# One row of the first load on eleven and nine DMA engines instead of sixteen, in a softmax with relative position bias

## The chip, the cores and the metric

The kernel runs on one core of a Trainium2 chip. The metric is device time in microseconds (us), the median of several runs. A core has compute engines that each run their own instruction stream: VectorE (DVE in the profile), ScalarE (ACT), GpSimd (POOL), TensorE (PE, not used here) and SyncE (SP), which here only issues transfers. Transfers between HBM and the on-chip memory (SBUF, 128 partitions) are carried by 16 DMA engines. Semaphores order everything: a transfer adds 16 to its semaphore when all of its data has landed.

## The reference

```
logits: (2, 8, 2112, 2112) float32      rel_bias: (8, 33) float32

rel  = pos[:, None] - pos[None, :]                  # 2112 x 2112
bias = rel_bias[:, clip(rel, -16, 16) + 16]         # one band matrix per head
x    = logits + bias[None]
x    = x - x.max(axis=-1, keepdims=True)
out  = exp(x) / exp(x).sum(axis=-1, keepdims=True)
```

There are 2 x 8 x 2112 = 33,792 rows of 2112 numbers (8448 bytes each). Each row gets a bias that depends only on the distance to its own position, and then a softmax. The input is 285 MB, the output as much.

## The kernel before, in words

Each of the 128 partitions owns 264 consecutive rows (ROWS). The kernel walks through them in 44 chunks of R = 6 rows per partition. A chunk is 128 partitions x 6 rows x 8448 bytes = 6336 KB, and one partition's part of it is contiguous in HBM. Four SBUF buffers X[0] to X[3] (NBUF) hold chunks in rotation; all work on a chunk is done in place.

For each chunk, VectorE adds the bias and takes the row's maximum in one instruction per row (line 167), ScalarE takes the exponential and the row's sum (line 176), VectorE inverts the sums (line 184) and scales the rows (line 188), half a chunk at a time. The bias is read from a strip F that is copied once per four chunks out of a longer band M in PSUM (`strip`, line 161). M is made in the first microseconds from `rel_bias`, by small VectorE instructions (lines 118 to 157).

SyncE issues all large transfers, in an order that is written out by hand. It first issues the first chunk as six loads of one row per partition (lines 88 to 91), then chunks 1 to 3 as one load each (lines 92 and 93, `load`, line 79). Then, in a loop, it waits for a chunk to be scaled and issues its store (`store`, line 83), waits until the store before it has landed, and issues the load that reuses that buffer (line 209). The last chunk is stored in two halves (lines 212 and 213). `take` (line 75) is the wait everywhere: it waits until a semaphore has reached a count and takes that count off again.

Two semaphores tell of the first chunk. The first five row loads count on `pre`, the sixth on `ld[0]`, which later loads of buffer 0 use too. VectorE waits for `pre` before its loop, and so before the first strip copy (line 191):

```
take(v, pre, 16 * (R - 1))
```

It then copies the strip, and waits for `ld[0]` (in `add`) before the first addition.

Of the kernel before, what the change touches and what calls it, by code (L numbers as in the profile page):

```python
# [15 lines left out]
def kernel(  # L16
# [6 lines left out]
    nc = tc.nc  # L23
    P = 128
    B, H, S, S2 = logits.shape
# [3 lines left out]
    ROWS = B * H * S // P  # L29
    PB = S // ROWS  # L30
    assert ROWS * P == B * H * S and PB * ROWS == S and PB == H == 8
    R = 6
# [5 lines left out]
    MW = S + ROWS - 1  # L38
    FW = S + STEP - 1
    BIG = 3.0e38  # L40

    io = ctx.enter_context(tc.tile_pool(name="io", bufs=1))
    X = [io.tile([P, R * S], FP32, tag=f"X{b}", name=f"X{b}") for b in range(NBUF)]
# [9 lines left out]
    def view(t, offset, dims):  # L53

        return bass.AP(tensor=t.tensor, offset=t.offset + offset, ap=[[list(t.ap[0])[0], P]] + dims)

    def rows(t, j, n):

        return bass.AP(tensor=t.tensor, offset=t.offset + j * S, ap=[[ROWS * S, P], [1, n * S]])

    with tc.tile_critical(no_gpsimd_drain=True):
        ld = [nc.alloc_semaphore(f"ld{b}") for b in range(NBUF)]
# [6 lines left out]
        pre = nc.alloc_semaphore("pre")  # L69
# [4 lines left out]
        def take(eng, sem, n):  # L74
            eng.wait_ge(sem, n).then_inc(sem, -n)  # L75
# [9 lines left out]
            ).then_inc(sem or st[b], 16)  # L85


        for r in range(R):
            nc.sync.dma_start(
                out=X[0][:, r * S : (r + 1) * S], in_=rows(logits, r, 1)  # L90
            ).then_inc(ld[0] if r == R - 1 else pre, 16)
        for n in range(1, NBUF):
            load(n * R, n)

# [4 lines left out]
            out=rbB,  # L99
            in_=bass.AP(tensor=rel_bias.tensor, offset=rel_bias.offset, ap=[[0, P], [1, H * W]]),  # L100
# [4 lines left out]
        v = nc.vector  # L105
# [22 lines left out]
        for m, op in ((eq, ALU.is_equal), (gt, ALU.is_gt), (le, ALU.is_le), (lt, ALU.is_lt)):  # L128
# [4 lines left out]
            out=view(F, 0, [[W, H], [1, W]]), in0=view(F, 0, [[W, H], [1, W]]),  # L133
# [9 lines left out]
            out=view(F, 0, [[W, PB], [1, W]]), in0=view(F, SC + 2 * PB, [[1, PB], [0, W]]),  # L143
# [7 lines left out]
            out=view(M, U, [[ROWS, PB], [1, W]]), in0=view(F, 0, [[W, PB], [1, W]]),  # L151
            in1=view(F, SC + 8 * PB, [[1, PB], [0, W]]), op=ALU.add))
        then(v.tensor_copy(out=view(M, U + W, [[ROWS, PB], [1, ROWS - W]]),  # L153
                           in_=view(F, SC + 7 * PB, [[1, PB], [0, ROWS - W]])))
# [8 lines left out]
        def add(b):  # L163
            take(v, ld[b], 16)
            for r in range(b * R, (b + 1) * R):
                x = X[b][:, (r - b * R) * S : (r - b * R + 1) * S]
                v.tensor_tensor_reduce(  # L167
                    out=x, in0=x, in1=F[:, STEP - 1 - r : STEP - 1 - r + S], scale=-1.0, scalar=BIG,
                    op0=ALU.add, op1=ALU.min, accum_out=nmax[:, r : r + 1],
# [18 lines left out]
                    v.tensor_scalar_mul(out=x, in0=x, scalar1=rec[:, r : r + 1]).then_inc(scaled, 1)  # L188

        v.sem_inc(dve, -done[0])  # L190
        take(v, pre, 16 * (R - 1))
        with nc.Fori(0, ROWS - STEP + 1, STEP, engines=[ENG.DVE]) as j:  # L192
            strip(j)
            take(v, dve, 1)
# [52 lines left out]
```

## Time and profile before

| | |
|---|---|
| median of 3 runs | 1331.21 us (1329.54 to 1332.16) |
| the profiled execution | 1330.01 us, its span 1328.2 us |
| VectorE busy | 976.7 us (74%) |
| ScalarE busy | 575.2 us (43%) |
| DMA queue of SP (q1) | 99.6% of 16 engines' span |
| moved over the span | 571.11 MB, 430 GB/s in the mean |
| loads of a chunk, issue to landing | 44.8 us median |
| stores of a chunk, issue to landing | 52.7 us median |

The span runs from the first to the last instruction of the profiled execution; its own time is a little longer. A DMA share is the mean busy share of the 16 DMA engines, so that 0.50 over a stretch can mean eight engines that work all the time. In lists of instructions, a trailing bracket names how long the engine was idle before, and what ended the wait. A `q` after an engine's name (SPq, DVEq) is its sequencer, which issues transfers and waits on semaphores.

### The profile page before, as it was taken

What the parts mean: (1) busy time and instruction counts of PE and PEld (TensorE: products, weight loads), DVE (VectorE), ACT (ScalarE), POOL (GpSimd) and SP (SyncE); (2) the same over time, 40 slices, a digit from 0 to 9 for tenths busy, and PEclk for the clock granted to TensorE, in tenths of its full rate; (3) what the DMA queues carried; (4) which work ended last, traced back from release to release, by engine and by line L of the source; (5) the groups of instructions that cost most, each with busy time, mean ns of one, the idle gap of its engine ahead of it and who ended that gap; (6) DMA issues with size and microseconds to landing.
All of it is one profiled execution on the core that took longest, in us unless ns stands there. A gap on an engine that the chain in (4) does not pass through costs nothing. (4 is left out here: it accounts for less than half of the span.)

```text
span 1328.2 us, 2456 instructions
## 1 busy us (share of the span) xinstructions
DVE 976.7 (74%) x911; ACT 575.2 (43%) x539; POOL 0.4 (0%) x6
## 2 busy tenths in 40 slices
DVE  6999667777877776687778777677877776677772
ACT  2574333444444343344444333434444343335441
POOL 0000000000000000000000000000000000000000
DMA  9999999999999999999999999999999999999998
GB/s 395 429 426 438 429 430 435 429 432 430 435 435 432 427 437 437 432 432 429 437 437 427 430 437 437 430 427 440 437 434 429 435 437 435 430 432 438 434 430 357
DMA packets 13682, 571.11 MB, mean 430 GB/s; under 512 B 1520, under 2 KB 1648, under 8 KB 1648
## 3 DMA queue, kind: packets, MB, share of 16 engines
q1 hardware_dynamic: 13536, 570.96, 99.6%
q10 hardware_dynamic: 144, 0.14, 0.1%
q14 instruction: 2, 0.02, 0.0%
HBM read 285.61 MB, written 285.47 MB: 430 GB/s over the span
## 5 line engine op out<-in xcount | busy, mean ns | idle before, releaser
L167 DVE CUSTOM_DVE_ANT_0 X<-X,F 128x2112 f32<-128x2112 f32 x264 | 605.2, 2354 | 302.1 <-DVEq L75 302.1
L176 ACT ACTIVATE X<-X,nmax 128x2112 f32<-128x2112 f32 x264 | 541.7, 2052 | 540.9 <-ACTq L75 519.2
L188 DVE TENSOR_SCALAR X<-X,rec 128x2112 f32<-128x2112 f32 x264 | 332.4, 1315 | 13.2
L176 ACT ACT_TABLE_LOAD x11 | 14.1, 1283 | 182.5 <-ACTq L75 182.5
L176 ACT ACTIVATION_READ_ACCUMULATOR X<-X,nmax 128x1 f32 x264 | 49.3, 187 | 0.0
L161 DVE COPY F<-M 128x2135 f32 x11 | 26.1, 2374 | 6.3 <-DVEq L75 6.3
L167 DVE DVE_READ_ACCUMULATOR2_ANT nmax<- 128x1 f32 x264 | 21.7, 82 | 0.0
L184 DVE RECIPROCAL rec<-tot 128x3 f32<-128x3 f32 x88 | 15.0, 170 | 0.0
L132 DVE TENSOR_TENSOR F<-F 128x264 f32<-128x264 f32 x1 | 0.4, 434 | 4.6 <-DMA F<-in_rel_bias_dram 4.6
L153 DVE COPY M<-F 128x1848 f32<-128x1848 f32 x1 | 2.1, 2077 | 0.0
L119 DVE TENSOR_SCALAR ip<-ip 128x8 int32<-128x8 int32 x1 | 0.2, 172 | 1.3 <-POOL ip L103 1.3
L136 DVE TENSOR_REDUCE rbS<-F 128x33 f32<-128x264 f32 x1 | 0.6, 611 | 0.0
L150 DVE TENSOR_TENSOR M<-F 128x264 f32<-128x264 f32 x1 | 0.4, 441 | 0.0
L142 DVE TENSOR_TENSOR F<-F,rbS 128x264 f32<-128x264 f32 x1 | 0.4, 428 | 0.0
L129 DVE TENSOR_SCALAR F<-F 128x8 f32<-128x8 f32 x4 | 0.4, 167 | 0.0
L155 DVE COPY M<-rbS 128x247 f32<-128x247 f32 x1 | 0.4, 406 | 0.0
L140 DVE TENSOR_SCALAR F<-F,rbS 128x8 f32<-128x8 f32 x1 | 0.2, 231 | 0.0
L146 DVE SCALAR_TENSOR_TENSOR F<-F,rbS 128x8 f32<-128x8 f32 x1 | 0.2, 225 | 0.0
L141 DVE TENSOR_SCALAR F<-F,rbS 128x8 f32<-128x8 f32 x1 | 0.2, 226 | 0.0
L147 DVE SCALAR_TENSOR_TENSOR F<-F,rbS 128x8 f32<-128x8 f32 x1 | 0.2, 219 | 0.0
L122 DVE TENSOR_TENSOR F<-ip 128x8 f32<-128x8 int32 x1 | 0.2, 168 | 0.0
L125 DVE TENSOR_TENSOR F<-ip 128x8 f32<-128x8 int32 x1 | 0.2, 168 | 0.0
(9 smaller groups left out, 1.2 us busy)
## 6 DMA issues: line engine op xcount, KB each, us to landing
X<-in_logits_dram SPq DMA_DIRECT2D x43, 6336.0 KB, 44.8
out_dram<-X SPq DMA_DIRECT2D x43, 6336.0 KB, 52.7
X<-in_logits_dram SPq DMA_DIRECT2D x6, 1056.0 KB, 12.0
out_dram<-X SPq DMA_DIRECT2D x2, 3168.0 KB, 21.1
F<-in_rel_bias_dram ACTq DMA_DIRECT2D x1, 132.0 KB, 6.2
```

The lines of the kernel that those rows point to most:

```text
L129: then(v.tensor_scalar(out=m, in0=dp, scalar1=0.0, scalar2=None, op0=op))
L132: then(v.tensor_tensor(out=view(F, 0, [[W, H], [1, W]]), in0=view(F, 0, [[W, H], [1, W]]), in1=view(F, SC + 3 * PB, [[1, H], [0, W]]), op= ...
L136: then(v.tensor_reduce(out=rbS[:, :], in_=view(F, 0, [[1, W], [W, H]]), axis=mybir.AxisListType.X, op=ALU.add))
L142: then(v.tensor_tensor(out=view(F, 0, [[W, PB], [1, W]]), in0=view(F, SC + 2 * PB, [[1, PB], [0, W]]), in1=view(rbS, W - 1, [[0, PB], [-1, ...
L150: then(v.tensor_tensor(out=view(M, U, [[ROWS, PB], [1, W]]), in0=view(F, 0, [[W, PB], [1, W]]), in1=view(F, SC + 8 * PB, [[1, PB], [0, W]] ...
L153: then(v.tensor_copy(out=view(M, U + W, [[ROWS, PB], [1, ROWS - W]]), in_=view(F, SC + 7 * PB, [[1, PB], [0, ROWS - W]])))
L155: then(v.tensor_copy(out=M[:, 0:U], in_=low.to_broadcast([P, U])))
L161: v.tensor_copy(out=F[:, :], in_=M[:, bass.ds(ROWS - STEP - j, FW)]).then_inc(dve, 1)
L167: v.tensor_tensor_reduce(out=x, in0=x, in1=F[:, STEP - 1 - r : STEP - 1 - r + S], scale=-1.0, scalar=BIG, op0=ALU.add, op1=ALU.min, accum_ ...
L176: nc.scalar.activation(out=x, in_=x, func=EXP, scale=-1.0, bias=nmax[:, r : r + 1], accum_out=tot[:, r : r + 1],).then_inc(expd, 1)
L184: v.reciprocal(out=rec[:, r0 : r0 + HALF], in_=tot[:, r0 : r0 + HALF]).then_inc(inv, 1)
L188: v.tensor_scalar_mul(out=x, in0=x, scalar1=rec[:, r : r + 1]).then_inc(scaled, 1)
```

## The change

The sixth row of the first chunk is loaded by two transfers in place of one: partitions 0 to 109, and partitions 110 to 127. They carry the same bytes to the same places. The 128-partition transfer has eight partitions for each of 16 DMA engines; the one of 110 runs on eleven engines with ten partitions each, the one of 18 on nine engines with two each. The first of the two counts on `pre`, which VectorE awaits before the strip copy, and the second on `ld[0]`, so that `pre` now stands for 16 x 6. Everything behind is as before.

```diff
+    MOST = 11 * 10
...
-        for r in range(R):
+        for r in range(R - 1):
             nc.sync.dma_start(
                 out=X[0][:, r * S : (r + 1) * S], in_=rows(logits, r, 1)
-            ).then_inc(ld[0] if r == R - 1 else pre, 16)
+            ).then_inc(pre, 16)
+        for p0, p1 in ((0, MOST), (MOST, P)):
+            nc.sync.dma_start(
+                out=X[0][p0:p1, (R - 1) * S : R * S],
+                in_=bass.AP(
+                    tensor=logits.tensor, offset=logits.offset + (p0 * ROWS + R - 1) * S,
+                    ap=[[ROWS * S, p1 - p0], [1, S]],
+                ),
+            ).then_inc(ld[0] if p1 == P else pre, 16)
...
-        take(v, pre, 16 * (R - 1))
+        take(v, pre, 16 * R)
```

## The prediction

> **What bounds the kernel now.** I read the page's busy shares and slices first, then its queues, then the stretches at both ends, and last what the issuing queue waits for.
>
> ```profile
> span 1328.2 us, 2456 instructions
> ...
> DVE 976.7 (74%) x911; ACT 575.2 (43%) x539; POOL 0.4 (0%) x6
> ...
> DMA  9999999999999999999999999999999999999998
> ...
> q1 hardware_dynamic: 13536, 570.96, 99.6%
> ```
>
> No compute engine is near full, while the 16 DMA engines are at work for 99.6% of the span: one queue of loads and stores, never empty until the last slice. The stretches say how fast it runs (columns: stretch, its length, DVE, ACT and POOL busy, clock, DMA share, GB/s).
>
> ```profile
> 7.00:17.00 10.00, 4.93 (x11) 0.00 (x0) 0.00 (x0) 1.00 1.01 427
> ...
> 900.00:1300.00 400.00, 297.38 (x275) 179.09 (x169) 0.00 (x0) 1.00 1.00 434
> ```
>
> 434 GB/s over sixteen engines is 27.1 GB/s each. There is no idle engine time in the body, so a byte put on one engine costs that engine its full time, and the kernel ends when the slowest of the 16 ends. That they do not end together is what the last microseconds show.
>
> ```profile
> 1320.00:1321.00 1.00, 0.00 (x0) 0.00 (x0) 0.00 (x0) 1.00 0.88 380
> 1321.00:1322.00 1.00, 0.00 (x0) 0.00 (x0) 0.00 (x0) 1.00 0.53 228
> 1322.00:1323.00 1.00, 0.00 (x0) 0.00 (x0) 0.00 (x0) 1.00 0.47 203
> 1323.00:1324.00 1.00, 0.00 (x0) 0.00 (x0) 0.00 (x0) 1.00 0.41 177
> 1324.00:1325.00 1.00, 0.00 (x0) 0.00 (x0) 0.00 (x0) 1.00 0.35 152
> 1325.00:1326.00 1.00, 0.00 (x0) 0.00 (x0) 0.00 (x0) 1.00 0.18 76
> 1326.00:1327.00 1.00, 0.00 (x0) 0.00 (x0) 0.00 (x0) 1.00 0.06 25
> 1327.00:1328.00 1.00, 0.00 (x0) 0.00 (x0) 0.00 (x0) 1.00 0.00 0
> ```
>
> Every engine has the same bytes in this kernel. Yet from 1321 to 1322 only 0.53 x 16, about 8.5, are still working, and in the last busy microsecond 0.06 x 16, one. So half of the engines end near 1321 and the other half straggle, the last to about 1327, 6 us later. The seven shares sum to 2.88 us: had all sixteen ended together, that would have been at 1320 + 2.88 = 1322.9, 4.1 us earlier. Where the stragglers lose it is seen in the queue that issues the loads. A load is issued as soon as the store before it on its buffer has landed on the last engine, so these starts follow the slowest engine (the view is the timeline of SP's own queue: start, length, name).
>
> ```profile
> 157.14 0.35 SPq L79 DMA_DIRECT2D X<-in_logits_dram  x1
> ...
> 278.19 0.35 SPq L79 DMA_DIRECT2D X<-in_logits_dram  x1
> ...
> 908.83 0.35 SPq L79 DMA_DIRECT2D X<-in_logits_dram  x1
> ...
> 1237.77 0.35 SPq L79 DMA_DIRECT2D X<-in_logits_dram  x1
> ```
>
> One chunk, a load and a store, takes 328.94 / 11 = 29.90 us over the last eleven, 630.64 / 21 = 30.03 over the 21 before them, and 121.05 / 4 = 30.26 over the four before those. At 29.90 throughout, the slowest engine would have been 1080.63 - 36 x 29.90 = 4.2 us earlier. Straggling is gained bit by bit in the first two thirds of the run.
>
> **The change part by part.** *The split.* The sixth row of the first chunk goes from 128 rows of 8448 bytes on 16 engines, 8 on each, to 110 on eleven (10 each) and 18 on nine (2 each). Some engines get 10 + 2 = 12 rows, four more than before, and the five that the eleven leave out are freed of up to 8. Price of a row: 427 GB/s / 16 = 26.7 GB/s, so 8448 bytes take 0.317 us. Four more rows: **+1.27 us** on an engine; eight fewer: -2.53 us. Nothing gives the 1.27 back, since every later transfer has equal shares for all sixteen and no engine waits for work.
>
> The trace before has no transfer on part of the engines, and which nine of the sixteen the 18 rows take is not in it. [...]
> [...]
>
> *Who is last.* With 8.5 engines ending within the first microsecond and the rest spread over five more, the end moves by what the last engine is given. If it is one with 12 rows: 1327 + 1.27. If it is a freed one: its end falls by 2.53, and another straggler decides. Ends of the range from this term: +1.27 and -2.1 us (the latter worked out under the rivals). I take +1.27: seven or eight stragglers cannot all be among five freed engines, and more engines are charged than freed.
>
> *A transfer more.* One more issue on SP's queue and one more set of completion counts.
>
> ```profile
> L89 SPq DMA_DIRECT2D X<-in_logits_dram x6: 388/514/647, 1.0 to 3.7; - x6
> ...
> 0.97 3.33 SPq L89 DMA_DIRECT2D X<-in_logits_dram  x6
> 4.34 1.80 SPq L79 DMA_DIRECT2D X<-in_logits_dram  x3
> ```
>
> An issue takes 0.51 us; the three large loads behind it are issued from 4.85 instead of 4.34 us. The engines then still hold the six rows (VectorE waits for the last of them until 21.12, in the rows of the next part), so this is hidden. Its completions cost nothing that I can find in a row: between 0 and one issue, 0.5 us; I take 0.
>
> *The first chunk's compute.* VectorE's first strip waits for `pre`; that now includes the 110-row part.
>
> ```profile
> 18.43 2.38 DVE L161 COPY F<-M 128x2135 f32 x1 [6.25 <-DVEq L75]
> 21.12 2.36 DVE L167 CUSTOM_DVE_ANT_0 X<-X,F 128x2112 f32<-128x2112 f32 x1 [0.31 <-DVEq L75]
> ```
>
> Today the strip starts when row five is in, and runs while row six arrives. After: ten rows' time later, 18.43 + 10 x 0.317 = 21.6, and the first addition at 21.12 + 3.2 = 24.3 us; the 18-row part lands 0.63 us after the 110 and is covered by the strip's 2.38 us. So every instruction of VectorE and ScalarE on the first chunks is 3.2 us late, and with them the first stores.
>
> ```profile
> 43.01 22.23 SPq L83 DMA_DIRECT2D out_dram<-X  x2
> 81.12 0.36 SPq L79 DMA_DIRECT2D X<-in_logits_dram  x1
> 86.56 0.34 SPq L83 DMA_DIRECT2D out_dram<-X  x1
> ...
> L79 SPq DMA_DIRECT2D X<-in_logits_dram x43: 349/349/652, 4.3 to 1237.8; - x43
> DMA to landing us min/median/max: 30.0/44.8/60.3
> ```
>
> The first store is issued at 43.0 and would be at 46.2; the third preload, issued near 5.9 us and slowest of all loads with 60.3 us, holds the engines until about 66. The second store (65.2, then 68.4) has the first one ahead of it until 81.1. Covers: 20 and 12.7 us against 3.2. The delay is then absorbed, as VectorE waits 302.1 us in all for loads. Cost 0; with the cover gone it would be the 3.2 us.
>
> ```profile
> L167 DVE CUSTOM_DVE_ANT_0 X<-X,F 128x2112 f32<-128x2112 f32 x264 | 605.2, 2354 | 302.1 <-DVEq L75 302.1
> ```
>
> *Straggling itself.* The freed engines run 12 rows, 3.8 us, ahead of the charged ones from the start. Whether this makes fewer or more of the losses is not shown by any row; it is bounded by taking away the 4.2 us of the slowest engine and by that amount once more. I take 0, because losses are over by 909 us although half the engines then straggle by microseconds, with 434 GB/s: running out of step is not in itself dear.
>
> [...]
>
> **The sum.** 1.27 + 0 + 0 + 0 = +1.3 us. The profiled execution took 1330.01 us (its span of 1328.2 and 1.8 around it), 1.2 us under the median of 1331.21; its own forecast is 1331.3, and against the median **1332.5**. That is 0.1%, inside the 0.2% (2.7 us) which is about what a measurement of this kernel can tell from no change.
>
> **The rivals.** *Faster: fewer losses.* If engines lose time because all sixteen turn from load to store nearly at once, the 3.8 us stagger stops it. For: losses end once they are spread. Against: they go on for 900 us with the spread growing. The slowest would get back up to 4.2 us and pay 1.27 where it is charged: -2.9, or 4.1 us from the tail's even end: 1327.1 to 1328.3. It needs over 3.9 us of loss gone to count as faster for a charged engine.
>
> *Freed engines are the last ones.* Then the last ends at 1327 - 2.53 = 1324.5; a straggler from about 1324.2 that is charged two rows (0.63 us) ends near 1324.9. Gain 2.1 us: 1329.1, still within 0.2%. For: seven or eight stragglers, and at least seven engines that are not charged four rows. Against: nothing ties them to the same engines.
>
> *Slower: the charged engines become the stragglers.* Being late at the turn would be what costs time; up to nine engines are now late from the first chunk. The price is 1.27 and the 4.2 us of losses a second time: +5.5, 1336.7 us. It decides from 1.4 us of added loss, a third of those of today. For: the losses of today come to half of the engines only and add up there. Against: the last third, 29.90 us a chunk, has stragglers and no loss.
>
> *It does not do what it says*: the parts spread evenly after all, or the rows hide: 1331.2.
>
> *The first chunk's delay reaches the queue*: +1.27 + 3.2 = +4.5, 1335.7; it needs 12.7 us of cover to vanish.
>
> **How the numbers follow.** Forecast 0.34, freed engines last 0.08, nothing done 0.03: same 0.45. Charged engines straggle 0.29 and first chunk 0.02: slower 0.31. Fewer losses: faster 0.24. The likeliest case alone has 1330.5 to 1334.5 (its zero terms up to 2 us either way). The range to hold 8 in 10 takes in the price of both large rivals: 1327 to 1337.
>
> **What would show it.** Right: the tail still about 6 to 7 us long, its last engine 1.3 us later; early in it (near 1319 to 1321) some five engines already done; chunks of 29.90 us at the end; strip at about 21.6 and first store near 46.2 us. Fewer losses: load issues 29.90 apart from the second hundred us on and a short tail. More losses: 30.2 or more well past 300 us, and a tail over 8 us. Wrong in the cover: a DMA share below 0.95 between 60 and 90 us.

## The result, and the profile after

The changed kernel takes 1335.50 us in the median of 7 runs (1334.69 to 1335.98), the kernel before 1330.66 us in 7 runs (1329.28 to 1332.16). The ratio is 1.0037, with a 95% interval of 1.0025 to 1.0048: slower by 4.9 us (the medians are 4.84 apart, which some expectations below give as 4.8). The forecast was 1332.5 us, slower by 1.3. The measured time lies in the wide range of 1327 to 1337, but outside the 1330.5 to 1334.5 of the likeliest case, and the loss is nearly four times the sum. The profiled execution took 1335.5 us, with a span of 1333.7 us, 5.5 us over that of before.

The kernel after, page and stretches (the columns are those of the stretches in the prediction):

```profile
DVE 976.7 (73%) x911; ACT 575.2 (43%) x539; POOL 0.4 (0%) x6
...
DMA  9999999999999999999999999999999999999997
GB/s 335 437 435 429 429 436 433 432 436 432 424 435 436 430 438 433 429 435 435 429 436 438 430 429 438 429 435 435 436 429 432 430 438 433 435 430 435 429 436 339
...
q1 hardware_dynamic: 13540, 570.96, 99.5%
```

The engines look as busy as before. But the first of the 40 slices moved 335 GB/s, where it was 395 before. Busy engines that move less: the loss must be looked for in GB/s, not in the busy share. A finer cut of the same kernel shows where.

```profile
7.00:17.00 10.00, 4.93 (x11) 0.00 (x0) 0.00 (x0) 1.00 1.01 428
17.00:20.00 3.00, 0.00 (x0) 0.00 (x0) 0.00 (x0) 1.00 1.10 276
20.00:23.00 3.00, 0.00 (x0) 0.00 (x0) 0.00 (x0) 1.00 1.23 253
23.00:26.00 3.00, 0.23 (x1) 0.00 (x0) 0.00 (x0) 1.00 0.90 273
...
130.00:400.00 270.00, 199.75 (x185) 119.40 (x113) 0.00 (x0) 1.00 1.00 432
400.00:900.00 500.00, 363.53 (x335) 211.60 (x199) 0.00 (x0) 1.00 1.00 433
900.00:1300.00 400.00, 295.66 (x272) 178.62 (x168) 0.00 (x0) 1.00 1.00 433
```

From 17 to 26 us, while the parts of 110 and 18 partitions run, the sixteen engines together move 250 to 280 GB/s, at a busy share of 0.9 and more (a share over 1 comes of counting a piece where it starts). Before and after that they are near the 433 GB/s of the body: 428 from 7 to 17 us, 418 from 26 to 30.

The trace also keeps the start and the length of each DMA packet, which here is one row, or one partition's piece of a chunk (50,688 bytes). In the kernel before, the 128 packets of the sixth row took 0.319 us in the median, and a piece took 1.87 to 1.88. In the kernel after, the packets of the same row took 0.585 us in the median. Five engines have no share in either part and begin the load of chunk 1 between 17.2 and 17.7 us; their first pieces, of an ordinary transfer to 128 partitions, took 3.19 to 3.48 us. So the parts are slow, and they slow engines that do not carry them.

Over the first 60 us, kernel before and kernel after:

```profile
0.00:60.00 60.00, 46.80 (x57) 26.51 (x25) 0.42 (x6) 1.00 0.97 408
```

```profile
0.00:60.00 60.00, 39.60 (x50) 20.57 (x20) 0.42 (x6) 1.00 0.96 377
```

31 GB/s less over 60 us are 1.86 MB, and at the 433 GB/s of the body that is 4.3 us of the 4.9. This one number, the bytes missing after 60 us, is given for all the runs below. The tail of the kernel after:

```profile
1324.00:1325.00 1.00, 0.00 (x0) 0.00 (x0) 0.00 (x0) 1.00 1.00 431
1325.00:1326.00 1.00, 0.00 (x0) 0.00 (x0) 0.00 (x0) 1.00 0.36 152
1326.00:1327.00 1.00, 0.00 (x0) 0.00 (x0) 0.00 (x0) 1.00 0.35 152
1327.00:1328.00 1.00, 0.00 (x0) 0.00 (x0) 0.00 (x0) 1.00 0.35 152
1328.00:1329.00 1.00, 0.00 (x0) 0.00 (x0) 0.00 (x0) 1.00 0.35 152
1329.00:1330.00 1.00, 0.00 (x0) 0.00 (x0) 0.00 (x0) 1.00 0.24 101
1330.00:1331.00 1.00, 0.00 (x0) 0.00 (x0) 0.00 (x0) 1.00 0.18 76
1331.00:1332.00 1.00, 0.00 (x0) 0.00 (x0) 0.00 (x0) 1.00 0.06 25
```

The main group now ends together near 1325, where it was near 1321: 4 us later. Behind it 0.35 x 16, about six, straggle over 6 to 7 us, much as before. No engine has ended before 1325: the lead of the engines that were freed of rows is gone.

### The profile page after: what moved, and what is told of

It is laid out like the page before. It is cut to its first block, busy times and chain, and to the rows that moved or that the text cites. A ratio compares the mean times of both kernels' runs of the same rounds, so it can differ in the third digit from the quotient of the medians.

```text
span 1333.7 us, 2457 instructions
## 1 busy us (share of the span) xinstructions
DVE 976.7 (73%) x911; ACT 575.2 (43%) x539; POOL 0.4 (0%) x6
```

## The experiments

Theories: **places** (a transfer to part of the partitions makes engines meet in the same part of SBUF, and all slow down while it runs), **counts** (only the number of rows on an engine matters), **late compute** (VectorE's late start reaches the end). Ratios are to runs of the kernel before on the same chip.

| kernel | ratio (95%) | GB/s, first 60 us | missing bytes, us | bytes added, us | measured, us |
|---|---|---|---|---|---|
| before | 1 | 408 | 0 | 0 | 0 |
| the change | 1.0037 (1.0025 to 1.0048) | 377 | 4.3 | 0 | +4.9 |
| e_cols | 0.9998 (0.9989 to 1.0007) | 408 | 0 | 0 | -0.3 |
| e_dve_late | 1.0000 (0.9991 to 1.0009) | 408 | 0 | 0 | 0 |
| e_64_64 | 1.0013 (1.0004 to 1.0022) | 389 | 2.6 | 0 | +1.7 |
| e_112_16 | 1.0014 (1.0005 to 1.0023) | 394 | 1.9 | 0 | +1.9 |
| e_mid | 1.0015 (1.0006 to 1.0024) | 394 | 1.9 | 0 | +2.0 |
| e_44_44_40 | 1.0039 (1.0025 to 1.0053) | 375 | 4.6 | 0 | +5.2 |
| e_two_rows | 1.0081 (1.0064 to 1.0098) | 345 | 8.7 | 0 | +10.8 |
| e_even | 1.0039 (1.0026 to 1.0053) | 405 | 0.4 | 5.15 | +5.2 |
| e_skew | 1.0111 (1.0095 to 1.0126) | 352 | 7.8 | 5.15 | +14.8 |
| e_src | 1.0114 (1.0097 to 1.0131) | 352 | 7.8 | 5.15 | +15.2 |
| e_low32 | 1.0073 (1.0056 to 1.0090) | 374 | 4.7 | 3.75 | +9.7 |
| e_step4 | 1.0032 (1.0021 to 1.0042) | 408 | 0 | 3.75 | +4.3 |

Missing bytes are (408 - GB/s) x 60 us / 433 GB/s; bytes added are those of an extra load, at 433 GB/s; measured is (ratio - 1) times the median of before (1329.4 to 1331.2 us).

**A transfer more, and a late start.** The sixth row as two transfers of 128 partitions, half a row each:

```diff
+        for c in range(2):
+            nc.sync.dma_start(
+                out=X[0][:, (R - 1) * S + c * S // 2 : (R - 1) * S + (c + 1) * S // 2], ...
```

> The sixth row is loaded by two transfers of all 128 partitions, each half a row wide: a transfer more, as in the change, but every engine keeps its eight partitions and its bytes. Shared places (an engine writes to partitions that another engine is writing to, and both slow down): 0, within 1.5 us of before. Uneven counts alone (12 rows against 8, at any price): 0. Late first compute: 0 (strip at most 0.5 us later). If a transfer more in itself were dear: up to +4.8 us, as with the change.

And all loads as before, with VectorE held up:

```diff
         take(v, pre, 16 * (R - 1))
+        for _ in range(3):
+            v.tensor_copy(out=F[:, :], in_=M[:, ROWS - STEP : ROWS - STEP + FW]).then_inc(dve, 1)
+            take(v, dve, 1)
```

> All loads as before; VectorE copies the strip three more times ahead of its loop, so that the first addition starts 7.3 us later or a little more, as it does with the change. Late first compute: +4.8 us. Shared places and uneven counts: 0, within 1 us, as the queue of loads covers it (first store at about 50.5 us, engines busy to 66).

Neither moves the time. In the second the first addition starts at 28.70 us, in the changed kernel at 28.46. First the run with VectorE held up, then the kernel after:

```profile
26.00 2.38 DVE L161 COPY F<-M 128x2135 f32 x1 [0.47 <-DVEq L75]
28.70 2.36 DVE L167 CUSTOM_DVE_ANT_0 X<-X,F 128x2112 f32<-128x2112 f32 x1 [0.31 <-DVEq L75]
```

```profile
25.77 2.38 DVE L170 COPY F<-M 128x2135 f32 x1 [13.52 <-DVEq L76]
28.46 2.36 DVE L176 CUSTOM_DVE_ANT_0 X<-X,F 128x2112 f32<-128x2112 f32 x1 [0.31 <-DVEq L76]
```

So the late compute is real and costs nothing, and the loss is in the transfers.

**Even counts, other cuts.** The sixth row is loaded in parts as in the change, by a loop over a list of bounds, so that each of the 16 engines has eight rows in all. All parts but the last count on `pre`. Each run has one of these lists:

```diff
+        PARTS = [(0, 64), (64, 128)]               # e_64_64
+        PARTS = [(0, 112), (112, 128)]             # e_112_16
+        PARTS = [(32, 96), (0, 32), (96, 128)]     # e_mid
...
+            for p0, p1 in PARTS:
```

> The sixth row is loaded in two transfers, partitions 0 to 63 and 64 to 127, each on all 16 engines with four partitions an engine. Every engine has eight rows as before, so uneven counts say 0 us. [...] Late first compute alone: below +1 us.

> The sixth row is loaded in two transfers of 112 and 16 partitions, both on all 16 engines, seven partitions and one on each. Almost the cut of the change, with even counts. [...] Uneven counts: 0. If the change's loss were that of the cut and not of the counts at all: +4.8 us.

> The sixth row is loaded in three transfers, partitions 32 to 95 with four on each of 16 engines, then 0 to 31 and 96 to 127 with two on each. Every engine has eight rows, so uneven counts say 0. [...] A rate that falls with any transfer of fewer than 128 partitions: as the split at 64 or worse, +2 to +3 us.

All three lose about 2 us with perfectly even counts; counts alone said 0. The intervals of e_mid and e_64_64 (0.8 to 3.2 and 0.5 to 2.9 us) do not tell the middle 64 partitions from the halves. The packets do. In e_mid the first 64 rows to start, those of the middle partitions, take 0.319 to 0.326 us each, as in the kernel before, and the other 64 take 0.58 in the median. In e_64_64 all but six of the 128 rows take longer than 0.34 us, with 0.63 in the median. So 64 partitions can be loaded at 0.319 us a row, the rate of all 128: it matters which they are, and their number alone does not decide.

The cut of 112 and 16, nearly that of the change, loses 1.9 us against 4.9, so not the cut alone decides: with counts of 12 and 0 it loses more than twice as much, and already in the first 60 us (1.9 against 4.3 us of missing bytes).

**Uneven counts, another cut.**

```diff
+        PARTS = [(40, 84), (84, 128), (0, 40)]    # 11, 11 and 10 engines, four partitions each
```

> The sixth row is loaded in three transfers, partitions 40 to 83 and 84 to 127 on eleven engines, 0 to 39 on ten, four partitions on each engine each time. Ten engines carry 12 rows, one 8 and five none: counts are as uneven as in the change. Uneven counts at 0.319 us a row: +1.3 us. [...] Uneven counts with stragglers that they make: +4.8 us as with the change, however fast the rows are.

It loses 5.2 us, like the change. The rate is down from the first part on: 262 GB/s from 17 to 20 us and 192 from 20 to 23, and five pieces of the ordinary load that start beside it, at 17.3 to 17.7 us, took 4.05 to 4.21 us each. The loss is also what was given for uneven counts that make stragglers later, but 4.6 us of bytes are missing in the first 60 us already.

**The dose doubled.** Rows five and six both as 110 and 18 partitions.

> The fifth and the sixth row of the first chunk are both loaded as 110 and 18 partitions, the dose of the change doubled. Rate lost by all engines while such parts run: about twice the 4.3 us that the mean rate of the first 60 us gives for one row, +8 to +10 us, mean rate near 345 GB/s. A single cost of leaving the even pattern once, or of VectorE's late start: +4.8 us as with one row. Uneven counts at 0.319 us a row alone: +2.5 us.

```profile
0.00:60.00 60.00, 35.41 (x46) 16.63 (x16) 0.42 (x6) 1.00 0.97 345
```

345 GB/s, as forecast from the lost rate. The +10.8 us lie above the 8 to 10 that were forecast, by less than their interval (8.5 to 13.0). A cost that is paid once, at +4.8, is out.

**Uneven counts with an extra load.** To make the unevenness large, 44 partitions of buffer 3 are loaded once more than needed; in the control the same number of bytes goes evenly to 128 partitions. Each run has one of the first two added lines:

```diff
-        for n in range(1, NBUF):
-            load(n * R, n)
+        nc.sync.dma_start(out=X[3][40:84, :], in_=...).then_inc(x3, 16)                  # e_skew
+        nc.sync.dma_start(out=X[3][:, : R * S * 44 // P], in_=...).then_inc(x3, 16)      # e_even
+        load(R, 1)
+        load(2 * R, 2)
+        take(nc.sync, x3, 16)
+        load(3 * R, 3)
```

> The sixth row is loaded as before; behind it one more transfer loads 44 partitions, 40 to 83, of buffer 3 a first time, whose real load then waits for it. [...] A lead that is lost again, so that only the mean over 16 engines counts: 44 x 50,688 bytes at 433 GB/s, +5.15 us, with no engine ending more than 1 us ahead of the main group. [...]

> The same extra bytes as in the run with 44 partitions, but from all 128 partitions, evenly over 16 engines: +5.15 us by every theory, the price of bytes alone. If it comes out as the uneven one does, unevenness costs nothing of its own.

The even one costs its bytes, 5.2 us. The uneven one costs 14.8 us, 9.6 more for the same bytes. This stretch of it says most about the mechanism:

```profile
26.00:30.00 4.00, 4.00 (x3) 4.00 (x5) 0.00 (x0) 1.00 0.97 203
```

203 GB/s over 4 us are 16 pieces of 50,688 bytes, one on each of the sixteen engines. Eleven engines carry the extra load, four pieces each (SyncE waits for it until 36.3 us, about four times 3.9 us after 20); the other five are already in the ordinary load of chunk 1. Had these five gone on at 27.1 GB/s and the eleven at half of that, the sum would be 284 GB/s. So the ordinary load is slowed too. The packets agree: all 16 pieces of this stretch take 3.89 to 3.93 us, in place of 1.87.

And the lead is lost here as well: five engines had no part in the extra load, yet none of the sixteen ends ahead of the main group.

```profile
1334.00:1335.00 1.00, 0.00 (x0) 0.00 (x0) 0.00 (x0) 1.00 1.00 431
1335.00:1336.00 1.00, 0.00 (x0) 0.00 (x0) 0.00 (x0) 1.00 0.77 329
1336.00:1338.00 2.00, 0.00 (x0) 0.00 (x0) 0.00 (x0) 1.00 0.35 152
```

**HBM or SBUF.** The extra load of 44 partitions, but from one contiguous piece of HBM; and 32 partitions from the same addresses, once into neighbours and once four apart:

```diff
-                tensor=logits.tensor, offset=logits.offset + (40 * ROWS + 3 * R) * S,
-                ap=[[ROWS * S, 44], [1, R * S]],
+                tensor=logits.tensor, offset=logits.offset,
+                ap=[[R * S, 44], [1, R * S]],                                            # e_src
...
+        nc.sync.dma_start(out=X[3][0:32, :], in_=...).then_inc(x3, 16)                   # e_low32
+        nc.sync.dma_start(out=X[3][0:128:4, :], in_=...).then_inc(x3, 16)                # e_step4
```

> As the run with 44 extra partitions (40 to 83 of buffer 3 loaded once more than needed, +14.8 us), but the data that is loaded first lies in one piece in HBM, 44 x 50,688 bytes, instead of 2.2 MB apart. That first load is overwritten by the real one, so the result is unchanged. Slow because of where it is read in HBM: back to +5 to +7.5 us and pieces of 1.87 us. Slow because of where it is written in SBUF, or because part of the engines carry it: +14.8 us and pieces of 3.9 us, as before.

> An extra load of 32 neighbouring partitions, 0 to 31, of buffer 3, two pieces of 50,688 bytes on each of 16 engines; counts are even. By bytes alone +3.75 us. [...] If only a share of the engines were what slows: +3.75 us.

> [...] Places in SBUF: faster than the load into neighbours, at best +3.75 us with pieces of 1.87 us. Reading in HBM: the same as the load into neighbours, whatever that is.

Reading elsewhere changes nothing beyond the noise (+15.2 against +14.8 us, and the same 352 GB/s). Writing elsewhere changes nearly all. From 20 to 27 us, 32 neighbours and then 32 partitions four apart:

```profile
20.00:27.00 7.00, 6.67 (x6) 3.49 (x4) 0.00 (x0) 1.00 0.82 181
```

```profile
20.00:27.00 7.00, 6.69 (x6) 3.39 (x4) 0.00 (x0) 1.00 0.99 427
```

Same bytes, same source, same sixteen engines with two pieces each: 181 against 427 GB/s, +9.7 against +4.3 us. The pieces that start from 19 us until the extra load is done take 3.4 to 4.0 us with neighbours and 1.87 to 1.88 with partitions four apart. So in this pair the loss is on the side of SBUF and depends on which partitions are written. For the change itself the same cause is argued and not shown by a run of its own: its slow packets, the doubled dose and e_mid fit it, but no run loads the sixth row in uneven parts whose partitions lie apart. None of these kernels is faster than the kernel before by more than the noise.

## Why the prediction was right or wrong

That the time lies inside the range is luck as far as the sum goes: the range was made wide to hold the price of two large rivals. By the prediction's own measure of 0.2% the result is no longer "same" but slower (0.37%), for which it gave 0.31.

*What bounds it* was right: each byte more costs its time (e_even: 5.15 us of bytes, 5.2 measured), and no compute engine matters.

*The price of a row* is the step that failed. "427 GB/s / 16 = 26.7 GB/s, so 8448 bytes take 0.317 us" was read from transfers to all 128 partitions and used for parts of them. The packets of the changed row took 0.585 us in the median, nearly twice that price. The strip that waits for the 110 partitions was forecast for 21.6 us and came at 25.77: ten rows took 25.77 - 18.43 = 7.3 us to the last engine, 0.73 each. In place of +1.27 us on the charged engines, all sixteen together lost bytes worth 4.3 us. Eleven and nine of sixteen engines have at least four in common, so that some carry twelve rows wherever the nine lie; that all nine lie among the eleven is borne out by the five that begin chunk 1 at once. What a transfer to part of the partitions costs, no row of the kernel before had shown. The runs with an extra load had 181 GB/s with 32 neighbours, 0.42 of 433, and 427 GB/s with 32 partitions four apart, so the number of partitions alone does not set the rate. While the eleven engines of e_skew were at theirs, the pieces took 3.89 to 3.93 us in place of 1.87.

*Who is last*: the end moved by the main group (1321 to 1325), not by one charged engine. Counting rows on engines was the wrong account, since freed engines were slowed as well and their lead was lost. The sign "some five engines already done", early in the tail, did not come: the share is 1.00 at 1324 to 1325.

*A transfer more* at 0: right (e_cols). *First chunk's compute* at 0: right (e_dve_late), though the delay was 7.3 us and not 3.2. The first store came at 50.36 us instead of 46.2, with a DMA share of 1.00 behind it, so the cover held:

```profile
50.36 22.22 SPq L84 DMA_DIRECT2D out_dram<-X  x2
...
60.00:90.00 30.00, 29.40 (x30) 18.83 (x18) 0.00 (x0) 1.00 1.00 433
```

*Straggling itself* at 0: about right, 0.6 us of the 4.9 are not in the missing bytes. The issues of the loads in the kernel after say nearly the same:

```profile
161.31 0.35 SPq L80 DMA_DIRECT2D X<-in_logits_dram  x1
...
281.02 0.35 SPq L80 DMA_DIRECT2D X<-in_logits_dram  x1
...
912.23 0.35 SPq L80 DMA_DIRECT2D X<-in_logits_dram  x1
...
1242.93 0.35 SPq L80 DMA_DIRECT2D X<-in_logits_dram  x1
```

The first of these is 4.2 us later than in the kernel before, the last 5.2. But the sign of 29.90 us a chunk at the end did not come: the three stretches have 29.93, 30.06 and 30.06 us a chunk, where they had 30.26, 30.03 and 29.90. That goes with the counts. Over the same eleven chunks all nine profiles with even counts (before, e_cols, e_dve_late, e_64_64, e_112_16, e_mid, e_even, e_low32, e_step4) have 29.90 or 29.91, and all five with uneven counts (the change, e_44_44_40, e_two_rows, e_skew, e_src) 30.03 to 30.06. So the unevenness of the first microseconds is still felt after 909 us, against "losses are over by 909 us". It costs nothing on the whole: from the first of these issues to the last it is 1080.8 to 1081.6 us with uneven counts and 1079.1 to 1083.2 with even ones.

Two rivals ended near the result with the wrong cause. Charged engines that become the stragglers (+5.5 us) laid the loss into later turns from load to store, and 4.3 us of it are there within 60 us. The first chunk's delay that reaches the queue (+4.5 us, 1335.7) came nearest, and e_dve_late has all of that delay and loses nothing.

*Open*: whether part of the loss comes after 60 us where a part was long or the counts uneven (e_skew 1.9 us, e_two_rows 2.1, e_low32 1.2, each inside the interval of its run), how a lead is lost and why uneven counts lengthen the last chunks, and which partitions an engine takes in a partial transfer. The runs show that the place in SBUF matters (181 against 427 GB/s) and that engines outside the partial transfer are slowed too (3.19 to 3.48 us a piece in the change); how one engine's write holds up another's was not measured.

## What to carry to other kernels

A rate per engine that was read from transfers to all 128 partitions need not hold for a transfer to some of them (0.319 us a row there, 0.585 in the change), and a slow one can slow the others that run beside it (3.19 to 3.48 us a piece in place of 1.87). Where part of the partitions must be loaded, try to spread them (every fourth and not the first 32 was right in the one pair tried here, 427 against 181 GB/s), and judge it by GB/s over a stretch: the busy share was still 0.82 to 0.97 here with the rate at half or less.

## What the runs showed of the hardware that was not expected

- 32 neighbouring partitions: 181 GB/s; 32 partitions four apart: 427 GB/s, with the same source and engines.
- 64 partitions in one transfer: the middle ones, 32 to 95, at the full 0.319 us a row, the halves 0 to 63 and 64 to 127 at 0.63 in the median.
- An ordinary load of 128 partitions ran at half rate too while a partial one ran on other engines (3.9 us a piece on all sixteen, in place of 1.87).
- A stretch of uneven counts within the first 35 us goes with 30.03 to 30.06 us a chunk after 900 us, where even counts have 29.90 or 29.91; over the run the two even out.
- Five engines were spared 4 pieces of 50,688 bytes, and yet 1.3 ms later no engine ended ahead of the main group.
